# Seven inner products for P7 of the last six output blocks of a float32 pooling-mixer trunk

## The chip, the cores and the metric

The kernel runs on one core of a Trainium2 chip. The metric is device time in microseconds (us) of one execution, measured from outside; the span is the time from the first to the last instruction in the profile of one such execution. TensorE (PE) multiplies, VectorE (DVE) and ScalarE (ACT) do elementwise work and move results out of the accumulator memory (PSUM, eight banks of 128 x 512 float32), GpSimd (POOL) does small work and issues some transfers, SyncE (SP) issues most transfers (DMA). Every engine works through its own list of instructions in order and waits on semaphores of the others.

## The reference, cut to what matters

Only the pooling layer runs (DEPTH is 1), on x of 4096 rows and 1024 columns, all float32.

```python
def pool_mixer(h, in_w, group_w, group_b, scale, out_w):
    u, gate = jnp.split(h @ in_w, 2, axis=-1)
    pooled = jnp.stack([trailing_mean(ug[:, :, g], w) for g, w in enumerate((2, 4, 8, 16))], axis=2) - ug
    mixed = jnp.einsum('bsgc,gcd->bsgd', pooled, group_w) + group_b
    y = mixed.reshape(b, s, POOL_WIDTH) * scale * jax.nn.silu(gate)
    return y @ out_w

def reference(x, ...):
    h = x + pool_mixer(rms_norm(x, norm_w), ...)
    return rms_norm(h, final_norm_w)
```

The change touches only the last step: y (4096 x 1024) times out_w (1024 x 1024), plus x, and the final norm.

## The kernel before

**Products.** A float32 operand is split into a high part (a ScalarE copy to float32r) and a low part (a VectorE subtraction), and a product is three passes: high by high, high by low, low by high (`mm3`). Each large product is done as the seven products P1 to P7 of the Strassen-Winograd scheme, on sums and differences of quarters. The input projection runs in two phases over four blocks of 1024 rows each (kinds "a" and "b"), then the output projection (kind "o") runs over eight blocks of 512 rows, numbered b = 0 to 7 in the code and called blocks 1 to 8 here. In an output block the products come in the order P1, P7, P6, P2, P5, P4, P3, and one product is two halves (j = 0, 1: 128 rows each) of 12 matmuls, each half into one bank of 512 columns.

**Banks.** Four pairs of banks rotate from block to block: x (P1, then P2 on top), v (P7, P4), y (P6, P5, P3) and spare. After P1, ScalarE copies the two x banks to y, so that P6 accumulates on P1; P7 starts v anew, P5 accumulates on P6 in y, P4 on v and P3 on y.

**P2 of blocks 3 to 8 (b > 1) is already done as seven inner products** of half the size (a second level of the same scheme): `split_inner` forms four sums of quarters of the operand and splits the operand and the sums into two slots of the ring of four operand slots `ops`; `product_inner` does one inner product as 6 matmuls of 128 x 256. Their weights are quarters of P2's weights and four sums of them, formed once in block 2 by `load_inner` and `form_inner` in four kept tiles. The inner products use the x banks and the spare banks; six VectorE additions of 256 columns (`add_inner`) carry the parts from the spare banks to the rows.

**Eviction.** `evict_o` adds each finished bank to a tile of x rows that `load_h` loaded earlier (512 KB for each 128 rows): out of P7, P6, P2, P5, P4 and P3, two VectorE additions of 512 columns each. `finish` then takes a half of the block: two ScalarE squares with a row sum, a root, a reciprocal on VectorE, four small GpSimd operations, two VectorE multiplications by the factor and the norm weight, and two stores.

**Order.** The program text is the priority; a scheduler (the tile framework) orders each engine's list when the kernel is built. `advance` calls `split_o` one or two products ahead (`split_reach`), and the loads four ahead. Slots of memory are 11 tiles `st` and 8 tiles `vt`; four `st` tiles become the kept tiles of the inner weights. An operand slot of `ops` can be rewritten only when the last matmul that reads it is done: P1, P7, P6, P2 (two slots), P5, P4, P3 take eight slots, so each block goes round the ring twice, and P5 takes the slot that P7 had, P4 the slot that P6 had.

Of the kernel before, what the change touches and what calls it, by code (L numbers as in the profile page):

```python
# [64 lines left out]
def kernel(  # L65
# [55 lines left out]
    def renew(t):  # L121
        i = next(i for i, u in enumerate(sts) if u is t)
        return mem.tile([P, D], F32R, tag=f"st{i}", name=f"inner{i}")
# [514 lines left out]
    def load_inner():  # L638
        inner_w["raw"] = [take() for _ in range(2)]
        for h, u in enumerate(inner_w["raw"]):  # L640
            nc.sync.dma_start(out=u, in_=wod[P2][h])

    def form_inner(stage):

        pattern, sizes = "p (n k s a) -> p n k s a", dict(n=2, k=2, s=2)
        if stage == 0:
            us = inner_w.pop("raw")
            b11, b12 = (quarter(us[0], j) for j in range(2))
            b21, b22 = (quarter(us[1], j) for j in range(2))
            raw = inner_w["sums"] = [take(pattern, **sizes) for _ in range(2)]  # L650
            (t3, t2), (t1, t4) = ([r[:, n] for n in range(2)] for r in raw)
            sub(t3, b22, b12)
            add(t2, t3, b11)
            sub(t1, b22, t2)
            sub(t4, b21, t2)
            for u in us:
                give(u)
            return
        r = inner_w["sums"][stage - 1]
        hi, lo = (kept.pop().rearrange(pattern, **sizes) for _ in range(2))  # L660
        copy(hi, r)
        sub(lo, r, hi.bitcast(F32))
        give(r)
        for n, i in enumerate(((P7, P6), (P5, P4))[stage - 1]):
            inner_w[i] = [v[:, n] for v in (hi, lo)]
        for i, (h, j) in {P1: (0, 0), P2: (1, 0), P3: (1, 1)}.items():
            inner_w[i] = [quarter(w[P2][h][:, s], j) for s in range(2)]

    def split_inner(u):
# [8 lines left out]
        ts = [  # L678
            next_op("p (s g k j c) -> p s g j k c", s=2, g=2, k=2, j=2),
            next_op("p (s n k c) -> p s n k c", s=2, n=4, k=2),  # L680
        ]
        split(ts[0].rearrange("p s g j k c -> p s (g k) (j c)"), u)
        split(ts[1], v)
        give(v)
        t = {P1: ts[0][:, :, 0, 0], P2: ts[0][:, :, 1, 0], P4: ts[0][:, :, 1, 1]}
        t.update({i: ts[1][:, :, n] for n, i in enumerate((P7, P6, P5, P3))})
        return t

    def product_inner(i):

        t, sets = inner["t"], inner["sets"]
# [4 lines left out]
        for k in range(2):  # L696
            a = [t[i][:, s, k] for s in range(2)]
            b = [inner_w[i][s][:, k].rearrange("p s a -> p a s") for s in range(2)]
            ps = bank.rearrange("p (a s) -> p a s", s=2)[:, half * P : (half + 1) * P]
            for n, (x1, x2) in enumerate(((a[0], b[0]), (a[0], b[1]), (a[1], b[0]))):  # L700
                latest[0] = nc.tensor.matmul(  # L701
                    ps, x1, x2, start=i in (P1, P7) and k + n == 0, stop=k == 1 and n == 2,
                    skip_group_check=True,
                ).ins
# [11 lines left out]
    def product_out(i, t, sets, last):  # L716
# [153 lines left out]
    def load_h(b, half):  # L870
        for j in range(2):
            u = take("p (a b) -> p a b", a=2)
            r = b * TO + (1 - half) * TH + j * P
            nc.sync.dma_start(out=u.rearrange("p a b -> p (a b)"), in_=x[r : r + P, :])
            hs[b][half, j] = u

    def load_o(b, i):
        s = oxs[b]
        if i == P1:
            s["11"] = load_y(b, 0, 0)  # L880
        elif i == P7:
            s["21"] = load_y(b, 1, 0)
        elif i == P6:
            s["22"] = load_y(b, 1, 1)
        elif i == P2:
            s["12"] = load_y(b, 0, 1)
            load_h(b, 1)
        elif i == P5:
            load_h(b, 0)

    def split_o(b, i):
# [3 lines left out]
        t = next_op("p (s a b) -> p s a b", s=2, a=4)  # L895
        if i == P7:
            s["3"] = take("p (a b) -> p a b", a=4)
            sub(s["3"], s["11"], s["21"])
        elif i == P6:
# [123 lines left out]
    def evict_o(b, i, sets):  # L1023
# [4 lines left out]
        factors = []  # L1028
        if inner and i == P2:
            inner["rows"] = [hs[b][0, j][:, 0] for j in range(2)]  # L1030
            add_inner(0, (0, 0))
# [7 lines left out]
        for j in range(2):  # L1039
# [4 lines left out]
            u = hs[b][half, j][:, n]  # L1044
            last = final and i in (P4, P3)
# [14 lines left out]
            if last:  # L1060
                factors.append(late_factor(half, j, parts))
                if i == P4 and j == 1 or i == P3 and j == 0:
# [4 lines left out]
                    else:  # L1067
                        rows = partial.pop("waiting")
                        late_scalar(*rows, nc.scalar)
                        late_vector(*rows)  # L1070
        if final and i == P3:
# [50 lines left out]
    def run(n, between=None, behind=None, seeds=4):  # L1122
        kind, b, i = steps[n]
        sets = sets_of(kind, b)
        if kind == "o":
# [199 lines left out]
    def split_reach(kind, b, i):  # L1325
        return 2 if kind == "o" and (b, i) != (0, P1) else 1
# [13 lines left out]
    stages = (P6, P5, P4)  # L1340
    stages = (P6, P5, P4)

    for n in range(2, len(steps)):
# [17 lines left out]
        if kind == "o" and b == 1 and len(kept) < 4 and not inner_w:  # L1361
            while len(kept) < 4 and len(st.free) > 2:
                kept.append(st.keep())
            if len(kept) == 4:
                load_inner()
        elif kept:
            keep[0] = 0
        advance("split", n, split_step, split_reach)
        if kind == "o" and b == 1 and i in stages:
            with tc.issue_after(latest_split[0]), tc.issue_after(latest_copy[0]):  # L1370
                form_inner(stages.index(i))
# [94 lines left out]
```

## Time and profile before

| | us |
|---|---|
| median of 3 runs (least, greatest) | 911.81 (911.46, 912.35) |
| profiled execution | 911.49 |
| its span | 909.4 |
| TensorE busy | 900.5 (99% of the span) |
| VectorE busy | 739.7 (81%) |
| ScalarE busy | 462.7 (51%) |
| first matmul of an inner product (block 3) | at 702.23 |
| start of the last P4, after the last inner product (block 8) | at 892.00 |

All times below are us from the start of the span. A row of the timeline gives start, duration, engine, source line, operation, output and input, how many instructions are merged in the row, and in brackets how long the engine was idle before and what released it. The line of a helper (159 is a subtraction, 165 a ScalarE copy) stands for every caller, so what an instruction is shows from its tiles: `op` is an operand slot, `bank` a PSUM bank, `st` and `vt` memory slots. Durations of one engine's neighbours overlap a little, so the step from start to start is the price of an instruction in a full queue.

### The profile page before, as it was taken

What the parts mean: (1) busy time and instruction counts of PE and PEld (TensorE: products, weight loads), DVE (VectorE), ACT (ScalarE), POOL (GpSimd) and SP (SyncE); (2) the same over time, 40 slices, a digit from 0 to 9 for tenths busy, and PEclk for the clock granted to TensorE, in tenths of its full rate; (3) what the DMA queues carried; (4) which work ended last, traced back from release to release, by engine and by line L of the source; (5) the groups of instructions that cost most, each with busy time, mean ns of one, the idle gap of its engine ahead of it and who ended that gap; (6) DMA issues with size and microseconds to landing.
All of it is one profiled execution on the core that took longest, in us unless ns stands there. A gap on an engine that the chain in (4) does not pass through costs nothing.

```text
span 909.4 us, 11434 instructions
## 1 busy us (share of the span) xinstructions
PE 900.5 (99%) x4320; PEld 789.3 (87%) x4320; DVE 739.7 (81%) x885; ACT 462.7 (51%) x693; POOL 46.4 (5%) x124
## 2 busy tenths in 40 slices
PE   9999999999999999999999999999999999999997
PEld 7888888888888888888888888888888898888886
DVE  4889995985995997685786699599789888978786
ACT  7869547447436555255345445544424424335334
POOL 0020100100100000000000000000101001001000
PEclk9999999999999999999999999999999999999999
DMA  9987767677676454134626615627475464464332
GB/s 343 401 303 238 265 236 238 193 264 242 232 268 197 148 208 139 47 139 138 255 86 219 251 70 186 208 93 233 163 252 184 150 223 160 141 232 140 116 139 93
DMA packets 66807, 178.08 MB, mean 196 GB/s; under 512 B 6080, under 2 KB 23872, under 8 KB 66752
## 3 DMA queue, kind: packets, MB, share of 16 engines
q1 hardware_dynamic: 60176, 155.83, 49.7%
q0 software_dynamic: 5856, 20.46, 6.1%
q10 hardware_dynamic: 720, 1.06, 0.3%
q8 instruction: 34, 0.56, 0.2%
q14 instruction: 21, 0.17, 0.1%
HBM read 116.50 MB, written 60.83 MB: 195 GB/s over the span
## 4 chain that ended last, share of the span: by engine, by line
PE 91%; DMA 3%; DVE 3%; issue 1%; SPq 0%; ACT 0%; POOL 0%; DVEq 0%; ACTq 0%; POOLq 0%
PE bank L603 88%; PE bank L701 3%; DMA early<-in_wut 2%; DMA st<-in_x 1%; DMA st<-yd 1%; DVE vt L1051 1%; PE bank L406 1%; DVE op L159 1%; DVE st L159 0%; DVE vt L934 0%; ACT st L961 0%; DVE vt L162 0%; DVE vt L711 0%; SPq L370 0%; DVE st L1051 0%
## 5 line engine op out<-in xcount | busy, mean ns | idle before, releaser
L603 PE MATMUL bank<-op,w 128*128 128x512 f32 x2688 | 580.9, 379 | 0.0
L603 PEld LDWEIGHTS bank<-op,w 128*128 128x128 f32 x2688 | 507.9, 189 | 72.4 <-ACT bank L165 0.4
L603 PE MATMUL bank<-w,op 128*128 128x512 f32 (+1 forms) x1212 | 262.2, 377 | 0.0
L603 PEld LDWEIGHTS bank<-w,op 128*128 128x128 f32 x1212 | 226.0, 189 | 31.0
L159 DVE TENSOR_TENSOR op<-st,op 128x1024 fp32r<-128x1024 f32 x129 | 156.5, 1219 | 62.2 <-ACT op L165 61.7
L165 ACT ACTIVATE op<-st 128x1024 fp32r<-128x1024 f32 x129 | 134.7, 1052 | 142.0 <-PE bank L603 94.3
L159 DVE TENSOR_TENSOR op<-vt,op 128x1024 fp32r<-128x1024 f32 x43 | 52.3, 1218 | 20.7 <-ACT op L165 20.5
L165 ACT ACTIVATE op<-vt 128x1024 fp32r<-128x1024 f32 x43 | 45.1, 1052 | 44.6 <-PE bank L603 35.5
L165 ACT ACTIVATE vt<-bank 128x512 f32<-128x512 f32 x82 | 47.7, 593 | 39.1 <-PE bank L603 39.0
L159 DVE TENSOR_TENSOR st<-st,st 128x1024 f32<-128x1024 f32 (+1 forms) x43 | 46.7, 1108 | 2.7 <-ACT st L930 1.3
L165 ACT ACTIVATE bank<-bank 128x512 f32<-128x512 f32 x48 | 27.9, 580 | 35.4 <-PE bank L603 35.3
L1051 DVE TENSOR_TENSOR vt<-bank,vt 128x512 f32<-128x512 f32 (+1 forms) x55 | 36.9, 675 | 7.8 <-PE bank L603 7.5
L165 ACT ACTIVATE st<-bank 128x512 f32<-128x512 f32 x48 | 27.9, 595 | 28.9 <-PE bank L603 17.4
L755 DVE TENSOR_TENSOR_SCAN vt<-vt,window 128x1040 f32<-128x1040 f32 x16 | 38.1, 2379 | 2.8 <-ACT vt L165 2.7
L159 DVE TENSOR_TENSOR w<-st,w 128x1024 fp32r<-128x1024 f32 x25 | 30.2, 1219 | 11.7 <-ACT w L165 11.7
L207 POOL TENSOR_SCALAR oms<-oss 128x2 f32<-128x2 f32 x14 | 6.4, 454 | 569.6 <-ACT st L930 459.2
L165 ACT ACTIVATE w<-st 128x1024 fp32r<-128x1024 f32 x25 | 26.0, 1051 | 16.8 <-PE bank L603 10.8
L1051 DVE TENSOR_TENSOR st<-bank,st 128x512 f32<-128x512 f32 x42 | 28.4, 684 | 7.0 <-PE bank L603 6.9
L806 DVE SCALAR_TENSOR_TENSOR st<-vt,colt,st 128x512 f32<-128x512 f32 x46 | 32.5, 745 | 1.7 <-ACT st L165 1.6
L165 ACT ACTIVATE st<-st 128x1024 f32<-128x1024 f32 x16 | 16.9, 1059 | 29.8 <-DVE st L156 29.7
L801 DVE SCALAR_TENSOR_TENSOR vt<-vt,vt 128x1024 f32<-128x1024 f32 x24 | 29.3, 1221 | 0.3
L934 DVE SCALAR_TENSOR_TENSOR vt<-vt,ors,st 128x1024 f32<-128x1024 f32 x18 | 22.5, 1282 | 8.2 <-POOL ors L225 8.2
(134 smaller groups left out, 637.5 us busy)
## 6 DMA issues: line engine op xcount, KB each, us to landing
st<-in_x SPq DMA_DIRECT2D x30, 512.0 KB, 4.9
st<-in_xt SPq DMA_DIRECT2D x28, 512.0 KB, 5.9
sd<-st POOLq DMA_DIRECT2D x28, 512.0 KB, 4.5
vt<-in_x SPq DMA_DIRECT2D x27, 512.0 KB, 4.0
st<-sd SPq DMA_DIRECT2D x24, 512.0 KB, 4.3
yd<-st SPq DMA_DIRECT2D x23, 512.0 KB, 2.6
st<-yd SPq DMA_DIRECT2D x20, 512.0 KB, 4.5
out<-vt SPq DMA_DIRECT2D x18, 512.0 KB, 3.4
```

Source lines behind the costliest of these rows:

```text
L159: return nc.vector.tensor_tensor(out=dst, in0=a, in1=b, op=ALU.subtract)
L165: return nc.scalar.activation(dst, src, func)
L207: (nc.vector if on_vector and not first else nc.gpsimd).tensor_scalar(out=ms, in0=ss, scalar1=1.0 / D, scalar2=EPS, op0=ALU.mult, op1=ALU.add)
L406: latest[0] = nc.tensor.matmul(ps, a[:, kk, 2 * j + t, :], maps, start=t + m == 0, stop=t == 1 and m == len(pairs) - 1,).ins
L603: latest[0] = nc.tensor.matmul(ps, a, b, start=start and n == 0, stop=stop and n == 2, skip_group_check=True).ins
L701: latest[0] = nc.tensor.matmul(ps, x1, x2, start=i in (P1, P7) and k + n == 0, stop=k == 1 and n == 2, skip_group_check=True,).ins
L755: nc.vector.tensor_tensor_scan(out=sums_[:, HIST:], data0=flat[:, HIST:], data1=flat[:, HIST - win : 2 * end - win], initial=first_sum, op ...
L801: nc.vector.scalar_tensor_tensor(out=s[:, :, at : at + H], in0=s[:, :, at : at + H], scalar=1.0 / win, in1=v[:, :, HIST:], op0=ALU.mult, o ...
L806: nc.vector.scalar_tensor_tensor(out=sg[:, j], in0=s[:, j, at : at + H], scalar=bias_c[2 * grp + j], in1=sg[:, j], op0=ALU.add, op1=ALU.mult,)
L934: nc.vector.scalar_tensor_tensor(out=us[j], in0=us[j], scalar=rs[:, j : j + 1], in1=fw[0], op0=ALU.mult, op1=ALU.mult,)
L1051: partial["added"] = nc.vector.tensor_tensor(out=dst, in0=src, in1=dst, op=ALU.add).ins
```

## The change

P7 of blocks 3 to 8 is also done as seven inner products, but in place: all of them go into the v pair of banks, seen as four cells of 256 columns. Two cells are cleared ahead by ScalarE; ScalarE copies between cells, and two VectorE additions of 256 columns inside PSUM, do the sums that the scheme needs. The work comes in parts: the first part before the first half of P1, the second between its halves, the third in the step of P7, and the last inner product (P4) after P6. The operand's sums go to two tiles of their own (`own_op`), the operand itself to one slot of the ring. The evictions of P7 and P6 move behind the last part. P5 is split one product ahead, not two.

In all blocks but the last, P7, P6 and P2 (the first to write to their rows) leave their banks by ScalarE copies of 512 columns, and x is added to those columns later by accumulating transfers from GpSimd's queue (`add_h`); `load_h` loads only the columns that are still added to on VectorE. The inner weights are formed for P7 and P2 in block 2 and at the start of block 3, in eight kept tiles (two of them the own operand tiles) and in one quarter of each weight in place.

```diff
-    def form_inner(stage):
...
+    def sum_inner(i):
+        us = raws[i]
+        t1, t3 = (quarter(us[0], j) for j in range(2))
+        t4, t2 = (quarter(us[1], j) for j in range(2))
+        sub(t1, t3, t1)
+        sub(t3, t2, t3)
+        sub(t2, t2, t1)
+        sub(t4, t4, t2)
...
+    def split_weight(i, p):
...
+        copy(home[0], raws[i][p])
+        sub(home[1], raws[i][p], home[0].bitcast(F32))
+        inner_w[i][p] = home
...
+    def split_inner(u, own=False):
...
+        if own:
+            sums_op = [t.rearrange("p x (y k c) -> p (x y) k c", y=2, k=2) for t in own_op]
+            latest_copy[0] = copy(sums_op[0], v).ins
+            latest_split[0] = sub(sums_op[1], v, sums_op[0].bitcast(F32)).ins
...
+    def cell(n):
+        return seven["v"][n // 2][:, (n % 2) * 2 * P : (n % 2 + 1) * 2 * P]
+
+    def clear_seven(b):
+        seven["v"] = sets_of("o", b)["v"]
+        for n in (0, 3):
+            nc.scalar.activation(cell(n), eps.to_broadcast([P, 2 * P]), AF.Copy, scale=0.0)
+
+    def product_seven(part, b):
+        def into(i, n):
+            leaf(seven["t"], inner_w[P7], i, seven["v"][n // 2], n % 2)
+        if part == 0:
+            into(P5, 3)
+            into(P1, 0)
...
+            copy(seven["m5"], cell(3))
+            copy(cell(2), cell(0))
+        elif part == 1:
+            into(P6, 2)
+            into(P2, 0)
+            copy(cell(1), cell(2))
+        elif part == 2:
+            into(P7, 2)
+            into(P3, 1)
+            add(cell(3), cell(2), seven["m5"])
+            add(cell(1), cell(1), seven["m5"])
...
+        else:
+            into(P4, 2)
...
         for j in range(2):
+            if between:
+                between(j)
...
+    def add_h(b, half, n):
+        for j in range(2):
+            nc.gpsimd.dma_start(
+                out=hs[b][half, j][:, n],
+                in_=x[row_of(b, half, j), n * H : (n + 1) * H],
+                accum_op=ALU.add,
+            )
...
+            if not final and i in (P7, P6, P2):
+                copy(halved(u), plain(ps[j]))
+                continue
...
+        if kind == "o" and b > 1 and i == P1:
+            seven["t"] = split_up.pop(n + 1)
+            product_out(i, split_up.pop(n), sets, False, lambda j: product_seven(j, b))
+            evict_o(b, i, sets)
+        elif kind == "o" and b > 1 and i == P7:
+            product_seven(2, b)
+        elif kind == "o" and b > 1 and i == P6:
+            product_out(i, split_up.pop(n), sets, False)
+            product_seven(3, b)
+            evict_o(b, P7, sets)
+            evict_o(b, i, sets)
+        elif kind == "o":
+            if i == P3 and 0 < b < NBO - 1:
+                clear_seven(b + 1)
...
-        return 2 if kind == "o" and (b, i) != (0, P1) else 1
+        return 2 if kind == "o" and (b, i) != (0, P1) and not (b > 1 and i == P5) else 1
...
+    forming = {
+        (1, P7): lambda: (load_inner(P7),),
+        (1, P6): lambda: (sum_inner(P7), split_weight(P7, P5)),
+        (1, P2): lambda: (split_weight(P7, P6), split_weight(P7, P7)),
+        (1, P5): lambda: (split_weight(P7, P4), end_weights(P7), load_inner(P2)),
+        (1, P4): lambda: (sum_inner(P2),),
+        (1, P3): lambda: (split_weight(P2, P7), split_weight(P2, P6)),
+        (2, P1): lambda: (split_weight(P2, P5), split_weight(P2, P4), end_weights(P2)),
+    }
```

More of the change, by code (lines that the diff above doesn't have):

```diff
@@ L669, in split_inner, with load_inner @@
-    def split_inner(u):
+    raws = {}
+    def load_inner(i):
+        raws[i] = [take() for _ in range(2)]
+        for h, u in enumerate(raws[i]):
+            nc.sync.dma_start(out=u, in_=wod[i][h])
+    def sum_inner(i):
[6 more added lines that the diff above has]
+        sub(t4, t4, t2)
+        raws[i] = {P5: t1, P6: t2, P7: t3, P4: t4, "held": us}
+        inner_w[i] = {
+            p: [quarter(w[i][h][:, s], j) for s in range(2)]
+            for p, (h, j) in {P1: (0, 0), P2: (1, 0), P3: (1, 1)}.items()
+        }
@@ L695, in product_inner @@
         }.get(i, (sets["spare"][0], 0))
[L696 to L704, printed above, removed]
+        leaf(inner["t"], inner_w[P2], i, bank, half, i in (P1, P7))
     def add_inner(bank, *places):
@@ L886, in load_o @@
             s["12"] = load_y(b, 0, 1)
[L887 to L888 removed]
+            if b == NBO - 1:
+                load_h(b, 1)
+        elif i == P5 and b == NBO - 1:
             load_h(b, 0)
@@ L1070, in evict_o @@
                         late_vector(*rows)
+        if inner and i == P2:
+            add_inner(0, (0, 0))
+        if not final and i in (P7, P6):
+            add_h(b, half, n)
+        elif not final and i == (P5 if with_inner else P2):
+            add_h(b, 0, 0)
         if final and i == P3:
```

118 lines of the change are left out of this document (65 added, 53 removed).

## The prediction

> **What bounds the kernel now.** First the page: the busy times, and the shares of the chain that ended last.
>
> ```profile
> PE 900.5 (99%) x4320; PEld 789.3 (87%) x4320; DVE 739.7 (81%) x885; ACT 462.7 (51%) x693; POOL 46.4 (5%) x124
> ...
> PE 91%; DMA 3%; DVE 3%; issue 1%; SPq 0%; ACT 0%; POOL 0%; DVEq 0%; ACTq 0%; POOLq 0%
> ```
>
> TensorE is busy in 99% of the span and holds 91% of the chain, so time goes where matmuls go, or where TensorE is made to wait. Then the windows, one for each of blocks 3 to 7, cut where TensorE starts the block's first inner product: the shortest, the longest and the sum of the five (columns: length, then busy time and count of each engine).
>
> ```profile
> core 0: us, PE busy (x) PEld busy (x) DVE busy (x) ACT busy (x) POOL busy (x), PEclk, DMA share, GB/s
> ...
> 738.18:773.95 35.77, 35.77 (x188) 31.91 (x186) 29.48 (x39) 14.34 (x21) 3.51 (x10) 1.00 0.42 148
> ...
> 845.73:882.13 36.40, 36.03 (x187) 31.83 (x186) 30.50 (x40) 14.50 (x21) 1.95 (x10) 1.00 0.35 127
> sum 179.90, PE 179.53 PEld 159.29 DVE 152.60 ACT 72.08 POOL 12.51; mean PE 35.91 PEld 31.86 DVE 30.52 ACT 14.42 POOL 2.50
> ```
>
> TensorE fills these windows but for 0.37 us in the last. The shortest is 35.77 us, and the five together stand 179.90 - 5 x 35.77 = 1.05 us above five of it: that is all that waits cost now. VectorE, at 152.60 / 5 = 30.5 us, has about 5 us of idle time in a block, ScalarE (14.4) has 21. VectorE has little to give away. Then the timeline of TensorE in block 5.
>
> ```profile
> 773.95 1.50 PE L701 MATMUL bank<-w,op 128*128 128x256 f32 x12
> ...
> 777.30 2.76 PE L603 MATMUL bank<-w,op 128*128 128x512 f32 x12
> ...
> 784.05 26.07 PE L603 MATMUL bank<-w,op 128*128 128x512 f32 x120
> 809.96 1.50 PE L701 MATMUL bank<-w,op 128*128 128x256 f32 x12
> ```
>
> 30 inner matmuls of 256 columns take 777.30 - 773.95 = 3.35 us, 0.1117 each; 120 of 512 columns take 809.96 - 784.05 = 25.91, 0.2159 each. Last, the steps of the two engines that feed TensorE, in the same block: VectorE, then ScalarE.
>
> ```profile
> 773.09 1.21 DVE L159 TENSOR_TENSOR op<-vt,op 128x1024 fp32r<-128x1024 f32 x1
> 774.23 0.68 DVE L1051 TENSOR_TENSOR st<-bank,st 128x512 f32<-128x512 f32 x1
> 774.83 1.22 DVE L159 TENSOR_TENSOR st<-vt,st 128x1024 f32<-128x1024 f32 x1
> ...
> 791.50 0.42 DVE L156 TENSOR_TENSOR st<-st,st 128x256 f32<-128x256 f32 x1
> 791.84 0.42 DVE L159 TENSOR_TENSOR st<-st,st 128x256 f32<-128x256 f32 x1
> 792.17 0.16 DVE L210 RECIPROCAL ors<-otmp 128x2 f32<-128x2 f32 x1
> ...
> 793.55 2.48 DVE L934 SCALAR_TENSOR_TENSOR st<-st,ors,st 128x1024 f32<-128x1024 f32 x2 [0.63 <-POOL ors L225]
> 795.95 0.68 DVE L1051 TENSOR_TENSOR vt<-bank,vt 128x512 f32<-128x512 f32 x1
> ...
> 801.32 1.23 DVE L159 TENSOR_TENSOR op<-st,op 128x1024 fp32r<-128x1024 f32 x1 [2.30 <-ACT op L165]
> ...
> 810.16 0.69 DVE L1051 TENSOR_TENSOR vt<-bank,vt 128x512 f32<-128x512 f32 x1 [0.90 <-PE bank L603]
> ```
>
> ```profile
> 773.93 1.06 ACT L165 ACTIVATE op<-vt 128x1024 fp32r<-128x1024 f32 x1 [4.12 <-PE bank L603]
> ...
> 798.70 0.58 ACT L165 ACTIVATE bank<-bank 128x512 f32<-128x512 f32 x1
> 799.22 1.03 ACT L930 ACTIVATE st<-vt 128x1024 f32<-128x1024 f32 x1
> ...
> 800.25 1.04 ACT L165 ACTIVATE op<-st 128x1024 fp32r<-128x1024 f32 x1
> 801.20 0.28 ACT L206 ACTIVATE otmp<-oss,eps 128x2 f32<-128x2 f32 x1
> 801.38 0.57 ACT L165 ACTIVATE bank<-bank 128x512 f32<-128x512 f32 x1
> ```
>
> Steps from start to start. VectorE: 1.14 for 1024 columns (773.09 to 774.23), 0.60 for a bank of 512 (774.23 to 774.83), 0.34 for 256 (791.50 to 791.84), 1.20 for one of the two scalings (793.55 to 795.95), which begin 1.38 after the reciprocal (792.17), since four GpSimd operations lie between. ScalarE: 0.52 for a 512 copy (798.70 to 799.22), 0.95 for an operand copy of 1024 (800.25 to 801.20), 1.03 for a square and the reading of its sum (799.22 to 800.25), 0.18 for the root (801.20 to 801.38). Hops: from the reported end of an operand's high copy (800.25 + 1.04) to its low half 0.03 (801.32); from TensorE's end of a bank to VectorE 0.20 (809.96 to 810.16); to rewrite an operand slot that TensorE has done with, none (773.93, TensorE goes on at 773.95).
>
> **The change, part by part.** *TensorE.* In each of six blocks 24 matmuls of 512 columns (5.18 us) become 42 of 256 (4.69 us): 0.49 less, 2.9 us in all. A block without waits would take 35.28 us. [...]
>
> *VectorE.* Six evictions of 512 leave (6 x 0.60 = 3.6); four quarter sums, one low half of 1024 and two additions of 256 in PSUM come (4 x 0.34 + 1.14 + 2 x 0.34 = 3.2). So VectorE gains nothing worth naming. *ScalarE* gets one operand copy (0.95), six bank copies (6 x 0.52 = 3.1), three cell copies and two clears of 256 columns. Those have no row; between a 512 copy (0.52) and the root of two columns (0.18) I take 0.36, midway, as cost falls with columns: 1.8. That makes 14.4 + 5.9 = 20.3 of 35.3 us. No engine becomes the bound by its sum. What decides is the order, since each list is served in order. I follow a block of the steady kind (blocks 4 to 7 have one order in the changed lists).
>
> *Wait A, ahead of P5.* P5's operand takes the ring slot that P7's has. Before, TensorE left P7 a whole P6 earlier. Now P7's last inner product (6 matmuls) reads that slot after P6, and TensorE has only the 24 inner matmuls of P2 (2.68 us) and three of P5's on the high half (0.65) as cover. From P6's end, called M, ScalarE's list is: P4's operand copy (its slot was P6's) from M + 0.02 to 0.99, the copies of P7's and P6's second banks to 2.03, P5's high copy to 3.12 (reported end). Then the low half: 1.22, ends at 4.37, TensorE goes on at M + 4.42. TensorE wants it at M + 0.67 + 2.68 + 0.65 = 4.00. Wait A is 0.42.
>
> *Waits B and C, ahead of P7's and P6's operands in the next block.* Put zero where A ends. TensorE ends P4 at 11.05 (10 + 6 + 11 + 6 matmuls, then 24) and P3 at 16.23, does P7's first inner product to 16.90, 16 matmuls of P1 to 20.35, and then wants the high half of P7's sums. VectorE's list from P4's second bank: at 11.25 the eviction 0.60, an addition 1.14, P7's own low half 1.14, the reciprocal 0.12, a quarter sum 0.34, P3's first bank 0.60 (to 15.19); the scalings from 14.13 + 1.38 = 15.51 to 17.90; a quarter sum, P3's second bank and two more sums to 19.60. ScalarE copies the high half from 19.63 to 20.69: a wait of 0.40. VectorE's difference for P6 and two low halves (3 x 1.14) bring the low half of the sums to 23.02, TensorE wants it 0.16 sooner. Meanwhile ScalarE, after that high copy, has a square (1.03), P6's high copy (0.95), a square (1.03) and only then the copy of P1's first bank, done at 24.23, where P6 wanted it at 23.97 with the waits so far: 0.31 with the hop. B and C together cost 0.40 + 0.16 + 0.31 = 0.87.
>
> So a steady block takes 35.28 + 0.42 + 0.87 = 36.57, a loss of 1.3 in waits against a gain of 0.49. Four such blocks: 5.2 us. Block 3 and block 8 have their own order: block 3 also splits eight quarter weights beside its evictions, and in block 8 VectorE still evicts P7 and P6. For each I bound the waits by 0 and twice a steady block's, 2.6, and take 1.3.
>
> *Forming weights.* Four more quarter sums (512 each, 0.60) and eight splits of 512 in place of two of 1024 on VectorE: 2.4 + 4.8 - 2.3 = 4.9 us, in block 2, whose six evictions of 0.60 leave (3.6), as do those of block 1. They hide in VectorE's idle time; what is late next is block 3, counted above.
>
> *Transfers.* SP loses the loads of whole x rows. GpSimd issues six accumulating transfers of 256 KB a block.
>
> ```profile
> DMA to landing us min/median/max: 2.9/3.9/13.5
> ```
>
> ```profile
> 103.61 0.54 POOL L515 DMA_DIRECT2D sd<-st  x1 [1.11 <-DVE st L162]
> 104.75 0.54 POOL L515 DMA_DIRECT2D sd<-st  x1 [0.60 <-DVE st L162]
> ```
>
> An issue takes 0.54 and the next follows 1.14 after (103.61, 104.75); they lie before GpSimd's reciprocal steps, which have 6 us to spare. No accumulating transfer is in the trace. Bounds: 2.9, the least landing of GpSimd's stores, and 13.5, the greatest. I take 4, near the median of 3.9, since an accumulating transfer moves less than those stores but also reads its target. The one used soonest carries P7's second bank: its copy ends at M + 1.54, and P5's second eviction wants it 10 + 6 + 11 matmuls and a hop after A's end (5.4), at M + 9.8, so 8.3 us are there, and it costs nothing.
>
> *Sum*, against the profiled execution's 911.49: - 2.9 (matmuls) - 1.05 (the waits of the windows, taken as replaced) + 5.2 + 2.6 = 915.3. The median stands 0.3 above that execution: 915.7.
>
> **The rivals.** *TensorE alone decides (faster).* The hops are shorter than I add them, or ScalarE gets ahead: A needs 0.42 less and B and C 0.87 less. For it: VectorE's idle total stays 5 us a block and ScalarE's 15. Against it: both lists have their idle time after TensorE's ends, not before its wants. It decides once the waits of all six blocks stay below 2.9 + 1.05 - 1.8 = 2.1 us. Time: 911.8 - 3.95 = 908.
>
> *The accumulating transfers come late (much slower).* If a transfer takes more than the 8.3 us, VectorE stands at P5's second eviction and with it P7's operand behind; each us more costs one in five blocks. At the bound of 13.5 that is 5 x 5 = 26 us, but the median of the row is 3.9. At 10 us: 915.7 + 5 x 1.7 = 924.
>
> *About even.* The waits of the six blocks sum to about 4, half of what I add up: 910.0 to 913.6.
>
> **How the numbers follow.** Waits as worked out: 0.56, late transfers: 0.08; both slower. TensorE alone: 0.22. Even: 0.14. What can be told from no change is about 0.2%, 1.8 us. Faster 0.22, same 0.14, slower 0.64. My own case runs from 913.1 (blocks 3 and 8 without waits) to 920.3 (those blocks at 2.6 each, and cell copies at 0.52 in place of 0.36, three in line: 0.5 in each of four blocks). The range reaches down into the faster case, to 908.5, and up to 922; that leaves out part of both rivals.
>
> **What would show it.** In the trace after: inner matmuls at 0.112, windows from block to block of about 36.6 where 35.3 would be without waits; TensorE's idle rows before P5's fourth matmul (released by VectorE), before P7's first matmul on its sums (released by ScalarE) and before P6's second use of y; VectorE's busy time in a block unchanged near 30, ScalarE's near 20; accumulating transfers landing in 3 to 6 us. It is wrong if TensorE shows no idle rows there, if blocks 3 or 8 hold most of the loss, or if VectorE waits on a transfer.

## The result, and the profile after

The changed kernel takes 939.73 us (median; 938.84 to 940.61), the kernel before 911.63 in the same comparison: 1.0311 times as long, with a 95% interval of 1.0299 to 1.0324. The direction was forecast, the size was not: 28.1 us slower, where 915.7 and at most 922.0 were predicted. In the experiments below one run of `keep8` (1188 us) and one of `swap` (1601 us) went at a far lower clock than the others (0.753 and 0.556) and are left out of the medians.

The page of the changed kernel, busy times and the shares of the chain that ended last:

```profile
PE 911.5 (97%) x4428; PEld 795.5 (85%) x4428; DVE 739.6 (79%) x895; ACT 499.2 (53%) x777; POOL 84.2 (9%) x166
...
PE 68%; DVE 14%; DMA 8%; ACT 4%; issue 4%; POOL 1%; SPq 0%; DVEq 0%; POOLq 0%; ACTq 0%
```

TensorE's busy time rose by 11 us although its matmuls became cheaper, and its share of the chain fell from 91% to 68%; VectorE and transfers now hold 22% of it. So it is made to wait, and part of what it does runs slowly. The window of one of the steady blocks, cut where TensorE starts P7's first matmul on its sums (same columns as the windows before):

```profile
740.70:778.05 37.35, 36.36 (x205) 31.97 (x205) 29.92 (x42) 19.46 (x33) 8.52 (x16) 1.00 0.61 169
```

A steady block takes 37.35 us, where 36.57 was predicted and 35.77 was the shortest before. VectorE and ScalarE are as busy as forecast (29.9 and 19.5, against "near 30" and "near 20"). The share of the DMA engines was 0.35 to 0.52 in blocks 4 to 7 before and is 0.61 here. TensorE's timeline in one of these blocks, the rows on both sides of its two larger waits:

```profile
755.66 0.81 PE L603 MATMUL bank<-w,op 128*128 128x512 f32 x3
756.68 2.43 PE L603 MATMUL bank<-w,op 128*128 128x512 f32 x10 [0.21 <-DVE op L159]
...
773.69 3.62 PE L603 MATMUL bank<-w,op 128*128 128x512 f32 x16
778.05 0.49 PE L711 MATMUL bank<-w,inner 128*128 128x256 f32 x2 [0.74 <-ACT inner L165]
```

These are waits A (0.21 idle ahead of P5's fourth matmul, released by VectorE; 0.37 counted from where the row of three before it ends at 755.66 + 3 x 0.2158) and B (0.74 ahead of the sums; 0.91 from 773.69 + 16 x 0.2158 to 778.05). But four blocks at 37.35 are not 28 us. The rest lies in TensorE's rows of the other blocks: the end of block 1, the start and the middle of block 3, and block 8:

```profile
647.45 46.63 PE L603 MATMUL bank<-w,op 128*128 128x512 f32 x214 [2.19 <-DVE vt L1136]
697.20 0.49 PE L711 MATMUL bank<-w,op 128*128 128x256 f32 x2 [3.12 <-ACT op L165]
...
718.17 0.66 PE L711 MATMUL bank<-w,op 128*128 128x256 f32 x2 [1.96 <-ACT op L165]
...
904.85 0.94 PE L711 MATMUL bank<-inner,inner 128*128 128x256 f32 x6 [3.93 <-ACT bank L165]
...
908.90 1.49 PE L711 MATMUL bank<-inner,inner 128*128 128x256 f32 x6
910.18 1.49 PE L711 MATMUL bank<-w,inner 128*128 128x256 f32 x6
```

TensorE stood 2.19, 3.12, 1.96 and 3.93 us, and 1.42 once more at 908.10. And some of the rows behind these waits are slow. Windows of TensorE alone behind three of them (length, busy, granted clock, DMA share):

```profile
697.20:701.40 4.20, 4.20 (x20) 0.59 0.00 0
718.17:722.34 4.17, 4.17 (x14) 0.59 0.91 230
908.10:913.89 5.79, 5.79 (x31) 0.58 0.00 0
```

The granted clock was 0.58 to 0.59 on average in these 4 to 6 us: (1 - 0.59) x 4.20 + (1 - 0.59) x 4.17 + (1 - 0.58) x 5.79 = 5.9 us of TensorE's time went to matmuls that ran slowly after a wait. Two inner products at 908.90 and 910.18 start 1.28 us apart, 0.213 a matmul, where 0.112 is the usual price.

### The profile page after: what moved, and what is told of

It reads as the page before. It is cut to its first block, busy times and chain, and to the rows that moved or that the text cites. A ratio compares the mean times of both kernels' runs of the same rounds, so it can differ in the third digit from the quotient of the medians.

```text
span 938.8 us, 11903 instructions
## 1 busy us (share of the span) xinstructions
PE 911.5 (97%) x4428; PEld 795.5 (85%) x4428; DVE 739.6 (79%) x895; ACT 499.2 (53%) x777; POOL 84.2 (9%) x166
## 4 chain that ended last, share of the span: by engine, by line
PE 68%; DVE 14%; DMA 8%; ACT 4%; issue 4%; POOL 1%; SPq 0%; DVEq 0%; POOLq 0%; ACTq 0%
PE bank L603 66%; DVE op L159 4%; DVE vt L159 2%; DVE vt L1016 2%; DMA early<-in_wut 2%; ACT op L165 2%; DMA out<-vt 2%; PE bank L711 2%; DVE vt L1136 1%; ACT vt L1012 1%; DMA st<-in_x 1%; DMA st<-yd 1%; DMA vt<-wod 1%; DVE st L156 1%; DVE inner L159 1%
## 5 line engine op out<-in xcount | busy, mean ns | idle before, releaser
L159 DVE TENSOR_TENSOR op<-st,op 128x1024 fp32r<-128x1024 f32 x107 | 129.9, 1220 | 68.2 <-ACT op L165 67.8
L165 ACT ACTIVATE op<-st 128x1024 fp32r<-128x1024 f32 x107 | 111.7, 1051 | 72.0 <-PE bank L603 47.5
L165 ACT ACTIVATE op<-vt 128x1024 fp32r<-128x1024 f32 x65 | 68.4, 1056 | 78.0 <-DVE vt L159 27.0
L165 ACT ACTIVATE vt<-bank 128x512 f32<-128x512 f32 (+1 forms) x127 | 71.8, 583 | 54.9 <-PE bank L603 40.2
L159 DVE TENSOR_TENSOR op<-vt,op 128x1024 fp32r<-128x1024 f32 x65 | 79.2, 1220 | 24.0 <-ACT op L165 23.8
L946 POOL DMA_DIRECT2D vt<-in_x x39 | 34.4, 909 | 443.5 <-DVE vt L817 354.2
L165 ACT ACTIVATE bank<-bank 128x512 f32<-128x512 f32 (+1 forms) x60 | 31.9, 535 | 41.4 <-PE bank L603 33.7
L1012 ACT ACTIVATE vt<-vt 128x1024 f32<-128x1024 f32 x26 | 27.3, 1050 | 26.7 <-DVE vt L1136 26.3
L711 PE MATMUL bank<-w,op 128*128 128x256 f32 x216 | 33.0, 291 | 6.9 <-ACT op L165 6.9
L159 DVE TENSOR_TENSOR st<-st,st 128x1024 f32<-128x1024 f32 x32 | 38.0, 1216 | 0.9 <-ACT st L246 0.6
```

Source lines behind the costliest of these rows:

```text
L159: return nc.vector.tensor_tensor(out=dst, in0=a, in1=b, op=ALU.subtract)
L165: return nc.scalar.activation(dst, src, func)
L711: latest[0] = nc.tensor.matmul(ps, x1, x2, start=start and k + n == 0, stop=k == 1 and n == 2, skip_group_check=True,).ins
L946: nc.gpsimd.dma_start(out=hs[b][half, j][:, n], in_=x[row_of(b, half, j), n * H : (n + 1) * H], accum_op=ALU.add,)
L1012: nc.scalar.activation(junk, us[j], AF.Square, accum_out=ss[:, j : j + 1])
```

## The experiments

**Which part costs how much.** The change was taken apart. In `s0` no block makes P7 as seven, all else stays:

```diff
-        if kind == "o" and b > 1 and i == P1:
+        if kind == "o" and b < 0 and i == P1:
```

(and so at the other places with `b > 1` for P7). `s47` makes it 3 <= b < 7, `s48` 3 <= b < 8. `s0_noform` also leaves out the forming of P7's weights, with three kept tiles where the changed kernel has eight (its lines below); `keep8` leaves out the forming too, but keeps eight tiles, so the first pair of lines stays as it was:

```diff
-            while len(gathered) < 8 and st.free and ...
+            while len(gathered) < 3 and st.free and ...
     forming = {
-        (1, P7): lambda: (load_inner(P7),),
-        ...
+        (1, P6): lambda: (load_inner(P2),),
+        (1, P5): lambda: (sum_inner(P2),),
+        (1, P4): lambda: (split_weight(P2, P7), split_weight(P2, P6)),
+        (1, P3): lambda: (split_weight(P2, P5), split_weight(P2, P4), end_weights(P2)),
```

For `s0_noform`:

> As the kernel without seven inner products of P7, and P7's quarter weights aren't formed and only three tiles kept for P2's; copies by ScalarE and accumulating transfers stay. Shortage of slots: back at 911.5 to 913. Accumulating transfers: 917 to 925 still. Inner products' own order: 911.5 to 913.

For `keep8`:

> No block makes P7 as seven, and P7's quarter weights aren't formed, but eight row tiles are still kept out of the ring of slots (three of them used). The output is the reference's. If the smaller ring alone delays loads: 916 to 921, near the kernel that also forms (920.8). If the forming (four loads, sums and splits in block 2) costs it: 911 to 913, near the one that keeps three tiles (910.8).

For `s0`:

> No block makes P7 as seven (P7 as one product with the replaced weight quarter, so the output of blocks 3 to 8 isn't the reference's); first banks copied by ScalarE, accumulating transfers, forming of both weights and the eight kept tiles as in the changed kernel. Shortage of slots: 5 to 11 us over the kernel before, 917 to 923, lost in blocks 1 to 3. Accumulating transfers: slow everywhere, 917 to 925, spread over all blocks. Inner products' own order: 911.5 to 913.

For `s47`:

> P7 as seven inner products in blocks 4 to 7 only; blocks 3 and 8 make it as one product (with a weight quarter that the forming has replaced, so their output isn't the reference's); all else as in the changed kernel. Shortage of memory slots (eight kept tiles and two weights formed in block 2): blocks 1 to 3 still lose most of their 13 us, the steady blocks 5.5, block 8 nothing: 925 to 930. The inner products' own order in blocks 3 and 8: these two fall away, 917. Accumulating transfers: as the shortage, 925 to 930.

For `s48`:

> The changed kernel with P7 as one product in block 3 (with the replaced weight quarter, so block 3's output isn't the reference's), as seven in blocks 4 to 8. If block 3's loss is its own inner products: 932 to 934. If it's the ring's, the forming's and the half clock's, which s0 has too: 935 to 938, and block 8 holds nearly all that lies between this kernel and the one with blocks 4 to 7 alone (927.3).

Measured, from the smallest part to the whole (ratio to the kernel before of the same comparison, with its interval):

| kernel | adds | median us | step | ratio |
|---|---|---|---|---|
| s0_noform | ScalarE copies, accumulating transfers | 910.75 | -0.3 | 0.9998 (0.9989 to 1.0008) |
| keep8 | five more kept tiles, unused | 916.78 | +6.0 | 1.0069 (1.0050 to 1.0087) |
| s0 | forming of P7's weights | 920.83 | +4.1 | 1.0105 (1.0090 to 1.0120) |
| s47 | P7 as seven in blocks 4 to 7 | 927.27 | +6.4 | 1.0176 (1.0159 to 1.0193) |
| s48 | in block 8 | 935.43 | +8.2 | 1.0270 (1.0252 to 1.0289) |
| after | in block 3 | 939.73 | +4.3 | 1.0311 (1.0299 to 1.0324) |

The kernels were not all timed in one comparison. By the ratios, times 911 us, the steps after the first are 6.5, 3.3, 6.5, 8.6 and 3.7 us. `s0_noform` takes the copies and the transfers by themselves out of the question, `keep8` fits the smaller ring, and `s0` and `s47` fit ring and transfers alike. The largest steps are block 8, which the forecast had at 0.8 (1.3 of waits less 0.49), and tiles that are only kept, which it had not listed. The steady blocks' own order, which it worked out, is the row of `s47`, 1.6 us a block. `s48` lies at the lower end of its second expectation, and its runs (933.94 to 938.24) reach into the first: block 3's own products cost 4.3 us on top of what `s0` has there.

**What the kept tiles do.** The timeline of SyncE's queue around the start of block 1, first of `s0_noform`, then of `keep8`: the y loads ahead of the next products.

```profile
625.50 0.37 SPq L929 DMA_DIRECT2D vt<-yd  x1
626.60 0.37 SPq L929 DMA_DIRECT2D st<-yd  x1
...
632.61 0.36 SPq L929 DMA_DIRECT2D st<-yd  x1
```

```profile
624.29 0.37 SPq L929 DMA_DIRECT2D st<-yd  x1
...
632.62 0.37 SPq L929 DMA_DIRECT2D vt<-yd  x1
633.08 0.60 SPq L929 DMA_DIRECT2D st<-yd  x1
```

The third of three loads is issued at nearly the same time, but with eight tiles kept the second is held back by 6 us, so that two run at once, beside the accumulating transfers. VectorE's row that waits for the last one, in `s0_noform` and in `keep8`:

```profile
639.02 1.22 DVE L159 TENSOR_TENSOR vt<-st,st 128x1024 f32<-128x1024 f32 x1 [5.11 <-DMA st<-yd]
```

```profile
642.20 1.23 DVE L159 TENSOR_TENSOR vt<-vt,st 128x1024 f32<-128x1024 f32 x1 [7.23 <-DMA st<-yd]
```

and TensorE's row behind it in `keep8`:

```profile
647.73 48.00 PE L603 MATMUL bank<-w,op 128*128 128x512 f32 x220 [2.38 <-DVE vt L1136]
```

VectorE has its operand at 642.20 in place of 639.02, what is queued behind it slides, a bank is evicted late, and TensorE stands 2.38 us where it had no wait. To take the changed kernel's other parts away altogether, `before8` keeps four more tiles in the kernel before, from block 3 on:

```diff
+        elif kind == "o" and b >= 2 and len(extra) < 4 and st.free and ...:
+            extra.append(st.keep())
```

> The kernel before the change, with four more row tiles kept out of the ring from block 3 on, unused. Nothing else is changed; the output is the reference's. If the ring's size matters by itself: 913 to 917. If it only matters with the changed evictions and transfers: 910.5 to 912.5.

917.55 us, a ratio of 1.0068 (1.0051 to 1.0085). Four unused tiles cost 6.2 us in a kernel that is otherwise the one before. VectorE's and TensorE's rows in a steady block:

```profile
773.71 0.69 DVE L1051 TENSOR_TENSOR st<-bank,st 128x512 f32<-128x512 f32 x1 [1.90 <-DMA st<-in_x]
...
779.32 1.23 DVE L159 TENSOR_TENSOR vt<-vt,vt 128x1024 f32<-128x1024 f32 x1 [2.51 <-DMA vt<-yd]
```

```profile
786.47 0.94 PE L701 MATMUL bank<-inner,op 128*128 128x256 f32 x6 [0.87 <-DVE vt L711]
```

VectorE waits for an x load and then for a y load, the additions of the inner products slide behind TensorE's want, and the block loses 0.87 us that it didn't lose before.

**What the accumulating transfers do.** `noadd` leaves out `add_h`'s transfers in the changed kernel, `keep8_noadd` in `keep8`:

```diff
     def add_h(b, half, n):
-        for j in range(2):
-            nc.gpsimd.dma_start(out=hs[b][half, j][:, n], in_=x[...], accum_op=ALU.add)
+        return
```

> The changed kernel without its accumulating transfers: x isn't added to the rows that ScalarE copies, so the output isn't the reference's. If the transfers and what they do to the other loads cost the time: 925 or less. If the shortage of slots or the inner products' order does: 936 to 940. Both theories leave about 1 us for VectorE's four waits on such transfers.

> Eight row tiles kept, no forming of P7's weights, P7 as one product, and no accumulating transfers (x isn't added to the copied rows, so the output isn't the reference's). If the smaller ring costs time whatever the transfers: 915 to 918, as with them (918.0). If it costs time because loads land later beside accumulating transfers: 909 to 912.

`noadd`: 931.38, ratio 1.0222 (1.0206 to 1.0237), so 8.4 us go with the transfers, between the two expectations. `keep8_noadd`: 914.09, ratio 1.0034 (1.0021 to 1.0047), 3.2 us below `keep8` by the ratios and between the two expectations as well. With enough slots the same transfers cost nothing (`s0_noform`). In `noadd` 8.3 of the 9.3 us between the two spans lie ahead of block 4: TensorE starts that block's first matmul on P7's sums at 732.38 instead of 740.70, and the next block's 37.36 us later, where the changed kernel takes 37.35. The rows of transfers from 600 us on, of the kernel before, of `after`, of `noadd` and of `s0_noform` (count, size, median us from issue to landing):

```profile
st<-yd SPq DMA_DIRECT2D x16, 512.0 KB, 4.8
vt<-yd SPq DMA_DIRECT2D x12, 512.0 KB, 4.8
```

```profile
vt<-in_x POOLq DMA_DIRECT2D x39, 256.0 KB, 6.5
vt<-yd SPq DMA_DIRECT2D x14, 512.0 KB, 6.8
st<-yd SPq DMA_DIRECT2D x14, 512.0 KB, 7.5
vt<-in_x SPq DMA_DIRECT2D x13, 256.0 KB, 2.9
```

```profile
vt<-yd SPq DMA_DIRECT2D x14, 512.0 KB, 4.4
st<-yd SPq DMA_DIRECT2D x14, 512.0 KB, 4.0
```

```profile
vt<-yd SPq DMA_DIRECT2D x15, 512.0 KB, 5.1
st<-yd SPq DMA_DIRECT2D x13, 512.0 KB, 5.5
```

An accumulating transfer of 256 KB takes 6.5 us to land, and beside such transfers a y load of 512 KB takes 6.8 to 7.5 in the changed kernel where it took 4.8 before and 4.0 to 4.4 without them. Neither the transfers nor the short ring does this alone: with the transfers and more slots (`s0_noform`) the y loads take 5.1 to 5.5, with eight tiles kept and no transfers (`noadd`) 4.0 to 4.4, with both (`keep8`) 7.5 to 8.6. With fewer slots loads started later and ran side by side (632.62 and 633.08 in `keep8`, above), and beside the transfers they then lasted longer. By the ratios the kept tiles cost 3.1 us without the transfers, the transfers nothing without the kept tiles, and both together 6.3: neither theory alone gives the measured times.

**Block 8.** ScalarE's row ahead of TensorE's wait of 3.93 us, and the stores on SyncE's queue, both in `after`:

```profile
904.01 0.38 ACT L165 ACTIVATE vt<-bank 128x256 f32<-128x256 f32 x1 [2.22 <-DMA out<-vt]
904.43 0.37 ACT L165 ACTIVATE bank<-bank 128x256 f32<-128x256 f32 x1
```

```profile
901.25 1.54 SPq L1020 DMA_DIRECT2D out<-vt  x2
```

The copy of P5's product (vt from bank, 256 columns) goes into a tile that `product_seven` takes afresh in block 8 only. ScalarE waits there for a store of rows to land (the last stores are those of block 7, issued from 901.25 on), and the next copy of a cell, for which TensorE waits, is behind it. `m5v` puts the copy into the tile of P7's operand sums, which is dead by then:

```diff
+        if hold:
+            seven["held"] = v
...
-                seven["held"] = take()
-                seven["m5"] = seven["held"][:, 0, 0 : 2 * P]
+                seven["m5"] = seven["held"][:, 0].rearrange("p k c -> p (k c)")
```

> The changed kernel; in block 8 alone the copy of the product by P5's sums goes into the tile of the operand sums, which is dead by then, and not into a fresh slot whose last store is still under way. If that slot holds block 8 up: the idle time of 3.93 us and the half-speed matmuls behind it go, 931 to 935. If the operands of block 8 come late anyway: 937 to 940.

932.57, ratio 1.0234 (1.0219 to 1.0249): 7.2 us less, for one destination. Not all of it is block 8's: the spans of the two profiled executions differ by 7.9 us, and 1.8 of these lie ahead of block 4 (738.89 against 740.70), where TensorE kept the full clock in the trace of `m5v` (1.00 from 697.42 to 701.62) and not in that of `after` (0.59 from 697.20 to 701.40). In TensorE's rows of `m5v` no wait is left between P6's matmuls and the inner products:

```profile
895.83 1.25 PE L603 MATMUL bank<-w,op 128*128 128x512 f32 x5
896.96 0.94 PE L714 MATMUL bank<-inner,inner 128*128 128x256 f32 x6
```

**The half clock.** `busy` put 14 matmuls of no use into P1 of block 8.

```diff
+                    for _ in range(14):
+                        latest[0] = nc.tensor.matmul(
+                            sets["spare"][1], seven["t"][P1][0][:, 0], w[P1][0][:, 0, 0], ...
```

> The changed kernel with 14 matmuls of 512 columns (3.0 us) of no use in P1 of block 8, written to a bank that is idle, so that TensorE works where it had 3.93 us of idle time; the wait itself is for a store's landing and isn't moved. If the half clock that follows (30 inner matmuls at 0.21 in place of 0.11 us) comes from the idle time: they run at 0.11, and the time is 936.5 to 938 although work was added. If the half clock has another cause, or the added work delays the chain: 939.5 to 943.

941.88, ratio 1.0344 (1.0311 to 1.0376). Inconclusive: the scheduler put them ahead of P6's matmuls, TensorE still stood 2.88 us behind these, and behind that wait six inner matmuls took 1.28 us (908.27 to 909.55), 0.213 each, as in `after`. `busy2` ties them to P6's second bank, so that they lie where the wait was:

```diff
             product_out(i, split_up.pop(n), sets, False)
+            if b == NBO - 1:
+                for _ in range(14):
+                    nc.tensor.matmul(sets["y"][1], warm[:, 0:P], warm, start=False, ...)
```

> The changed kernel with 14 matmuls of 512 columns (3.0 us) behind P6's product in block 8, where TensorE had 3.93 us of idle time; they add ones to a bank, so the output of that block isn't the reference's. If idle time brings the half clock: about 0.9 us of idle time is left, the 30 inner matmuls that follow run at 0.11 in place of 0.21 us, and the time is 936.5 to 938.5. If the half clock comes without it: 939.5 to 941.

938.41, ratio 1.0301 (1.0286 to 1.0316), 1.3 us under the changed kernel with 3 us of work more. TensorE's rows, and the window of the inner products behind:

```profile
899.19 3.01 PE L1228 MATMUL bank<-const-bfloat16-1.0 128*128 128x512 bf16 x13
903.97 0.94 PE L711 MATMUL bank<-inner,inner 128*128 128x256 f32 x6 [1.78 <-ACT bank L165]
...
906.09 0.94 PE L711 MATMUL bank<-inner,inner 128*128 128x256 f32 x6 [0.52 <-ACT bank L165]
906.87 0.83 PE L711 MATMUL bank<-w,inner 128*128 128x256 f32 x6
```

```profile
903.90:907.50 3.60, 3.01 (x24) 1.00 0.00 0
```

The inner products start 0.78 us apart (906.09 and 906.87), where it was 1.28 in the changed kernel, at a granted clock of 1.00. One execution alone doesn't settle this, since the clock stayed full behind some other waits too (3.44 us in `m5v`), and the 1.3 us are not clear of noise, as the two intervals overlap. The busy time says a little more: in the 3.41 us ahead of the half clock in `after` (902.67 to 906.08) TensorE was busy for 1.23 us; in `busy2` it was busy for 1.64 in the 3.41 us from 901.56 (counted as in the last section, from the end of a half clock near 652.4 in the same trace), and the clock stayed full behind them. The half clock was gone where part of the idle time was filled; that the idle time is its cause is my reading of these two traces.

**Waits A and B.** `swap` lets P5's operand take the slot of P6's and P4's that of P7's:

```diff
+        if b > 1 and i == P5:
+            turn[0] += 1
+            t = next_op("p (s a b) -> p s a b", s=2, a=4)
+            turn[0] -= 2
+        elif b > 1 and i == P4:
+            t = next_op("p (s a b) -> p s a b", s=2, a=4)
+            turn[0] += 1
```

> The changed kernel with one edit: P5's operand takes the ring slot of P6's and P4's that of P7's. If wait A is the read of P7's slot by its last inner product: the row before P5's fourth matmul (0.22 idle, 0.37 to the last one's end) goes, the period of blocks 4 to 7 falls by 0.4 to 0.5, 937 to 938 in all. If P5's operand is late by ScalarE's list and not by the slot: no change, 939 to 940.5.

The three executions took 933.21, 933.28 and 938.17, ratio 1.0260 (1.0231 to 1.0289), none of them within either range. The edit left no trace that can be compared, so the same edit was run on `m5v`, as `m5swap`:

> The changed kernel with block 8's copy in the dead tile (932.6 alone) and P5's operand in P6's ring slot. If wait A is the slot: the row of 0.22 us before P5's fourth matmul goes and the period of blocks 4 to 7 falls from 37.35 by 0.3 to 0.5: 930.5 to 931.5. If swapping slots moves more than that (the earlier run was 4 us under the changed kernel): 927 to 930.

935.31, ratio 1.0267 (1.0252 to 1.0282), above both expectations. The window of a steady block, and TensorE's rows in blocks 3, 4 and 8, of `m5swap`:

```profile
777.97:814.82 36.85, 36.09 (x204) 32.03 (x204) 29.90 (x42) 19.43 (x33) 8.44 (x16) 1.00 0.62 172
```

```profile
723.56 0.94 PE L714 MATMUL bank<-inner,op 128*128 128x256 f32 x6 [1.49 <-DVE vt L733]
...
740.42 0.49 PE L714 MATMUL bank<-w,inner 128*128 128x256 f32 x2 [1.28 <-ACT inner L165]
...
907.11 3.50 PE L603 MATMUL bank<-w,op 128*128 128x512 f32 x15 [1.86 <-DVE op L159]
```

Wait A's row is gone and a steady block takes 36.85, 0.50 less: A was the slot, and was priced right (0.42 and a restart). Yet the whole is 2.7 us slower than `m5v`, with blocks 3, 4 and 8 in other waits (rows above), and with 20 matmuls in block 3 that took 4.20 us behind a wait of 3.11 us (from 696.95), where the same 20 took 2.80 in `m5v` behind one of 3.44. How `swap` alone came to its times, without `m5v`'s edit, stays open. Gains of single edits don't add here.

`reach3` splits P7's operand and sums a step earlier, ahead of the scalings:

```diff
+        if kind == "o" and b > 2 and i == P7:
+            return 3
```

> The changed kernel with one edit: from block 4 on P7's difference, sums and operands are placed one step earlier in the lists, at P4 of the block before instead of P3. If wait B is the place of P7's sums behind the scalings in VectorE's list: the idle row before P7's first matmul on its sums (0.74) goes and the period of blocks 4 to 7 falls from 37.35 to about 36.4, 935 to 937 in all. If the loads that feed it (with eight tiles kept) come too late for that, or what was ahead comes late instead: 939 or more.

956.30, ratio 1.0490 (1.0472 to 1.0508), far on the second side. The waits of VectorE and TensorE in `reach3` (engine, line, for what; us in total, times, longest):

```profile
DVE vt L159 <- DMA st<-yd: 30.2, 6, 8.0
...
PE bank L711 <- DVE vt L730: 18.5, 5, 4.5
```

VectorE asks for the y loads a step sooner than they can be there, stands 30 us for them, and TensorE stands for VectorE's additions. So B didn't yield to this order. That it would with the kept tiles' slots free for the loads is argued, not tried. `steady` combined both edits:

> The changed kernel with two edits for the steady blocks: P5's operand takes P6's ring slot and P4's takes P7's (against wait A), and P7's operand and sums are split one step earlier, ahead of the scalings (against waits B and C). If A and B are what the two orders make of them: the period of blocks 4 to 7 goes from 37.35 to about 36.0, 933 to 936 in all. If other work on VectorE then comes late in their place: 37.0 or more, 938 to 941.

961.41, ratio 1.0543 (1.0522 to 1.0564), but the two edits clash: P7's operand of the next block is written into the slot that P4's still needs, so P4's product is made from it and comes behind it. It says nothing on A or B.

**The forming, later.** `late` forms P7's weights in block 3, keeps five of the eight tiles from there on, and makes P7 as seven from block 4 on:

```diff
+        (2, P7): lambda: (load_inner(P7),),
+        (2, P2): lambda: (sum_inner(P7), split_weight(P7, P5)),
+        ...
-            while len(gathered) < 8 and ...
+            while len(gathered) < (3 if b < 2 else 8) and ...
```

> P2's quarter weights are formed in block 2 as before the change, P7's only in block 3, with five of the eight tiles kept from block 3 on; P7 as seven in blocks 4 to 8. If both weights and all tiles in block 2 cost the time: blocks 1 to 3 lose little, blocks 4 to 7 some 6.4, block 8 some 10: 926 to 929. If forming costs as much wherever it lies: 935 to 940.

936.63, ratio 1.0277 (1.0260 to 1.0294): the second side, and level with `s48` (1.0270, the intervals overlap), which has the same blocks as seven and forms all in block 2: no saving by moving the forming is shown. TensorE still stands 2.03 us at the end of block 1, blocks 4 to 6 get waits of 1.3 to 2.3 us of their own, and block 8's 3.92 is there. No kernel of these beats the kernel before; `s0_noform` equals it.

## Why the prediction was wrong

*Right:* the direction; the matmuls' prices; that no engine becomes the bound by its sum; the place and the releaser of waits A and B, and A's price (0.42 forecast, 0.37 measured, 0.50 with the restart by `m5swap`).

*Mis-sized: waits B and C, and the restarts.* B was 0.40 + 0.16 and measured 0.91. A steady block came to 37.35 - 35.28 = 2.07 us of waits instead of 1.29. C shows as 0.2 us a block, in which weight loads of 512-column products wait for a bank copy of ScalarE (0.9 us over the four blocks; 0.31 was forecast). The rest of the 2.07, some 0.6, is spread in small pieces, such as 0.1 at a restart behind a wait (ten matmuls take 2.27 from 756.68 to 758.95, in place of 2.16), which the forecast had at nothing; it was not divided further. Four blocks: 6.4 measured (`s47` less `s0`), against 4 x (1.29 - 0.49) = 3.2. This is 3 of the 24 us that were missed.

*The step that failed: "Forming weights. ... They hide in VectorE's idle time".* Its sum was one of VectorE's time only. The step keeps eight of the 19 tiles where four were kept, so that 11 are left for loads, sums and rows in place of 15, and I gave that no price, though the change's own loop that keeps eight tiles stands in the diff. It is worth 6 us alone (6.3 by the ratio of `keep8`, 6.2 by that of `before8`), and the forming itself 3 to 4 more where 0 was put: together about 10 of the 24 us. That the two figures for the tiles agree is partly chance: TensorE waits 2.38 us at the end of block 1, 0.96 in block 3 and 0.73 in block 8 in `keep8`, but 0.8 to 0.9 five times from block 4 on in `before8`, which keeps its tiles only from block 3 on. The waits for transfers in the profile of before (VectorE for a y load, ScalarE for stores that held a slot) could have hinted that little was to spare:

```profile
ACT st L930 <- DMA out<-st: 3.9, 3, 2.2
...
DVE st L159 <- DMA st<-yd: 3.0, 1, 3.0
```

*"Blocks 3 and 8 ... bound the waits by 0 and twice a steady block's, 2.6".* They cost 4.3 and 8.2 with the matmuls' gain taken off, where 0.8 each was put: about 11 of the 24 us. The bound was taken from blocks with another order, and block 8's one tile that is only taken there was not followed to the store that holds its slot. The forecast named a loss in these blocks as what would make it wrong.

*Accumulating transfers "cost nothing".* The landing was 6.5 (4.1 to 8.7) instead of 4. VectorE did wait for one of them in each of blocks 4 to 7, 0.9 to 1.2 us ahead of an eviction (759.72 in the first), which the forecast had named as a sign of being wrong. But a steady block of `noadd` is no shorter (37.36), so there the price is indeed nothing, as it is with slots enough. But I asked only who waits for these transfers, and not what they do to others: y loads of 4.8 us became 6.8 to 7.5, and that is 3 us with the short ring (`keep8`) and 8.4 in the changed kernel.

*Not in the forecast: the clock.* TensorE spent 5.9 us more on matmuls at half clock behind waits of 2 to 4 us. This is part of the sums above, and how much of it reaches the end was not measured.

## What to carry to other kernels

Tiles that a change keeps are a cost of their own (6.2 us for four unused ones in `before8`): count the slots that are left for loads, and price the change as the loads starting later, before any engine's time. A transfer that costs nothing by its own landing can still lengthen the loads beside it, here where few slots were left (y loads of 512 KB from 4.0 to 4.4 us in `noadd` to 6.8 to 7.5 in the changed kernel). And in the first and the last block follow every tile that is taken only there to the store or load that last held its slot.

## What the runs showed of the hardware that was not expected

TensorE's clock fell to half behind single waits of 1.96, 3.12 and 3.93 us. In the trace of `after` the granted clock is 1.00 or 0.50, and up to the last matmul it is at half from 697.87 to 701.28, from 718.35 to 721.76 and from 906.08 to 912.91: 3.41, 3.41 and 6.83 us, with 17.07 and 184.32 us between them, all whole multiples of 3.413 (1, 1, 2, 5 and 54). So I count in stretches of 3.41 us from these points (in `m5v` from the half clock that starts near 924.5, after its last matmul). First the stretch of `after` that holds the wait of 1.96 us, with the one behind it, then the two stretches of `m5v` that share a wait of 3.44 us (length, busy, count, granted clock, DMA share, GB/s):

```profile
714.94:718.35 3.41, 1.45 (x7) 1.00 1.01 238
718.35:721.76 3.41, 3.41 (x11) 0.50 0.92 224
```

```profile
692.35:695.77 3.42, 1.63 (x8) 1.00 0.76 307
695.77:699.18 3.41, 1.76 (x13) 1.00 0.00 0
```

Before the half clocks of `after` TensorE at full clock was busy for 0.67 us (the stretch from 694.46), 1.45 (714.94) and 1.23 (902.67); the least that it was busy in such a stretch with the full clock behind it is 1.66 there (from 899.26). The two stretches of `m5v` above have 1.63 and 1.76, that of `busy2` has 1.64, all with the full clock behind them. The wait's length alone doesn't sort these cases: the half clock came behind 1.96 us in `after`, but not behind 2.19 in the same trace, nor behind 3.44 in `m5v`. That the busy time within a stretch decides is my estimate from these few; no run varied it by itself.

An accumulating transfer from GpSimd is dearer than its bytes: 256 KB land in 6.5 us, where a plain load of 256 KB by SyncE lands in 2.9 (both in `after`, rows above). No run separates the addition from the queue that issues it. Its issue holds GpSimd for 0.876 us (median of 39), where a plain store from GpSimd held it 0.54 in the kernel before.
